# Down products of a feed-forward block ordered by weight part, and the lower activations placed like the upper ones

## The chip, the cores and the metric

One core of a Trainium2 chip runs the whole program. The metric is device time in microseconds for one execution; the median of several runs counts.

## What is computed

Two transformer blocks over 256 tokens of width 1024 in float32, with seven stages: feed-forward, mixer, feed-forward in the first block, then twice a mixer and a feed-forward. Four of the seven are the same gated feed-forward, hidden width 2816:

```python
def _swiglu(x, w_gate, w_up, w_down):
    return (jax.nn.silu(x @ w_gate) * (x @ w_up)) @ w_down
```

The change touches only the last product, with `w_down`, in these four stages.

## The kernel before

**Precision in two parts.** TensorE gets every float32 operand as two tiles: an upper part (`wh`, `hh`, `xh`), which is the rounded copy, and a lower part (`wl`, `hl`, `xl`), which is the rest. A product of two operands is three matmuls: upper by upper, upper activation by lower weight, lower activation by upper weight.

**Weights.** All weights come through one stream (`Stream`, L45 on) in tiles of 128x1024. SP loads a raw tile, ScalarE casts it to `wh` (L89), VectorE subtracts to get `wl` (L94). Four raw tiles and six pairs `wh`, `wl` are in the ring. `take(n)` hands out the next n pairs and issues casts and subtractions for later ones, as far as the ring's pairs are no longer in use. VectorE's subtraction is followed by the load of a later raw tile.

**A feed-forward stage** (`ffn`, L615 on) has a first part and then ten blocks j = 1 to 10 of 256 hidden columns. A block multiplies by the gate weights (`gemm_b2`, lines 535 and 537: weights stationary, activations streamed, 512 and 256 columns), does the same for the up weights, forms silu(gate) x up in `sg`, and splits that into `hh` (ScalarE, L653) and `hl` (VectorE, L654). Then it calls `down` for the chunks of the block before, so that `hh` and `hl` have been ready for a whole block. The engines follow the order in which the code issues work.

**`down`** takes two weight tiles (four in the last call of a stage). The 256 tokens are two halves h, the 1024 output columns two banks b; four PSUM banks add up over the whole stage. Here the activations are stationary (128 columns are loaded into TensorE for each matmul) and 512 columns of weights are streamed. In the old order h is the outer loop, then tile i, then bank b, and for each of these `mm3` (L511 on) issues its three matmuls: (`hh`, `wh`), (`hh`, `wl`), (`hl`, `wh`). All of them are recorded at L523, and so are those of the mixers' products. A call with n=2 has 24. A stage has nine calls with n=2 and one with n=4.

**Places in SBUF.** A spacer of `WL_AT` = 192 bytes lies between the tiles `wh` and `wl`, and one of the same size, `gap3` (L651), between `hh` and `hl`. The other spacers (`gap2` from `HH_AT`, L622) bring `hh` to the same place in each stage. Modulo 512 bytes `wh` and `hh` begin at 160 and `wl` and `hl` at 352 in every feed-forward stage. All offsets within the tiles that a matmul uses are multiples of 512 bytes.

**Three other groups of products** appear in the rows. `gh` is the first product of a mixer, issued all (`xh`, `wh`), then all (`xh`, `wl`), then all (`xl`, `wh`), eight of each for a half of the tokens; in the first mixer `xh` lies at 160 and `xl` at 352. `wo<-hah` are output products of the first mixer, in the old order of three with activations `hah` and `hal`, which both lie at 160. In all of these, weights are streamed, 512 columns at a time, and activations are stationary. `gb` are the gate and up products.

Of the kernel before, what the change touches and what calls it, by code (L numbers as in the profile page):

```python
# [8 lines left out]
F32 = mybir.dt.float32  # L9
# [5 lines left out]
P = 128  # L15
# [12 lines left out]
WL_AT = 192  # L28
# [160 lines left out]
class Kern:  # L189
# [407 lines left out]
    def down(self, accs, chunk, n, act, cut=False):  # L597


        tiles = self.ws.take(n)  # L600
        last = chunk + n == 22
        b2 = [(0, slice(0, 512)), (1, slice(512, D))]
        for h in range(2):
            t = slice(h * P, (h + 1) * P)
            m = n - 2 if last else n
            cs = [b2[0], (2, slice(512, 768)), (3, slice(768, D))] if last and len(accs[h]) > 2 else b2
            for i, (b, c) in [(i, b) for i in range(m) for b in cs] + [(i, b) for b in cs for i in range(m, n)]:
                ah, al = act(chunk + i)
                wh, wl = tiles[i]
                k = chunk + i  # L610
                self.mm3(accs[h][b], [((ah[:, t], al[:, t]), (wh[:, 0, c], wl[:, 0, c]))],
                         k == 0 or b > 1 and i == 0, k == 21 or cut and b == h == 1 and k == 17)


    def ffn(self, gpre, gpost, coef, gnext, hooks=None, cut=False):  # L615
        nc = self.nc
        tt = nc.vector.tensor_tensor
        with self.tc.tile_pool(name="ffn", bufs=3) as fp:
            self.php = fp
            self.pair_xt = True  # L620
            self.nff = getattr(self, "nff", -1) + 1
            fp.tile([P, HH_AT[self.nff] // 4], F32, name="gap2", tag="gap2", bufs=1)  # L622
            hts = {}
            st = {}
            accs = None

            def act(c):
                hh, hl = hts[c // 2]
                return hh[:, c % 2, :], hl[:, c % 2, :]

            def first(h, mid):
                if h == 0:
                    st["w"] = self.ws.take(4)
                p = self.ps(f"fh{h}")
                t = slice(h * P, (h + 1) * P)
                w = st["w"]
                ops = [(self.xh[:, 2 * i + k, t], w[i][x][:, k, :]) for i in range(4) for x in range(2) for k in range(2)]
                ops += [(self.xl[:, k, t], w[k // 2][0][:, k % 2, :]) for k in range(8)]
                for n, (l, r) in enumerate(ops):
                    if mid and n == 24 - 12 // self.after:  # L640
                        mid()
                    nc.tensor.matmul(out=p, lhsT=l, rhs=r, start=n == 0, stop=n == 23)  # L642
                sg = fp.tile([P, S], F32, name="sgf", tag="sgf", bufs=2)
                nc.scalar.activation(out=sg, in_=p[:, 0:S], func=AF.Silu)
                tt(out=sg, in0=sg, in1=p[:, S:2 * S], op=ALU.mult)
                st[h] = sg

            def split(t, j):
                hh = fp.tile([P, 2, S], F32R, name="hh", tag="hh")
                if not hts:  # L650
                    fp.tile([P, WL_AT // 4], F32, name="gap3", tag="gap3", bufs=1)  # L651
                hl = fp.tile([P, 2, S], F32R, name="hl", tag="hl")
                nc.scalar.copy(out=hh, in_=t)  # L653
                tt(out=hl, in0=t, in1=hh.bitcast(F32), op=ALU.subtract)  # L654
                hts[j] = (hh, hl)

            def gather(t, banks):
                for c, p in enumerate(banks):
                    nc.scalar.copy(out=t[:, c, :], in_=p[:, 1, :])  # L659
                    tt(out=t[:, c, :], in0=p[:, 0, :], in1=t[:, c, :], op=ALU.add)  # L660

            self.enter(gpre, first)
            self.pair_xt = False
            self.gain(gnext)
            if gpost:
                self.gain(gpost)
            for j in range(1, 11):
                sg = fp.tile([P, 2, S], F32, name="sg", tag="sg", bufs=1)
                su = fp.tile([P, 2, S], F32, name="su", tag="su", bufs=1)
                gather(sg, self.gemm_b2())  # L670
                nc.scalar.activation(out=sg, in_=sg, func=AF.Silu)
                if j == 1:
                    p = self.ps("ft")
                    for c in range(2):
                        for h in range(2):
                            nc.tensor.transpose(p[:, c * S + h * P:c * S + (h + 1) * P], st[h][:, c * P:(c + 1) * P],
                                                self.ident)
                    split(p.rearrange("p (c t) -> p c t", c=2), 0)
                gather(su, self.gemm_b2())
                tt(out=sg, in0=sg, in1=su, op=ALU.mult)  # L680
                split(sg, j)
                for f in (hooks or {}).get(j, []):
                    f()
                if accs is None:
                    accs = [self.ps2("f0"), self.ps2("f1")]
                if j < 10:
                    self.down(accs, 2 * (j - 1), 2, act, cut)
            if cut:
                accs[1] += [self.ps("f1c")[:, 0:S] for _ in range(2)]
            self.down(accs, 18, 4, act)  # L690
            self.close(accs, gpost, coef)
# [1069 lines left out]
```

## Time and profile before

| what | value |
|---|---|
| median of 3 runs | 1098.65 us (1098.41 to 1099.42) |
| profiled execution, its own time | 1100.22 us |
| its span, first to last instruction | 1098.4 us |
| granted TensorE clock, mean share | 0.998 |
| TensorE busy | 1082.7 us, 99% |
| VectorE, ScalarE, GpSimd busy | 738.0, 598.3, 314.6 us |
| moved by DMA | 190.83 MB, mean 174 GB/s |

The profile is of one execution. Busy shares are means over stages; the chain of work that ended last says which engine's time adds up to the end. Matmuls are pipelined, so the duration of one overlaps the next: what one costs is the interval from its start to the next one's start, which the timeline shows.

### The profile page before, as it was taken

The page shows a single profiled execution, that of the slowest core. Times are in us where ns is not written, and L with a number is a line of the kernel's source. Part 1 is how long each engine was busy: PE and PEld are TensorE (multiplying, and loading weights), DVE is VectorE, ACT ScalarE, POOL GpSimd, SP SyncE. Part 2 cuts the span into 40 slices and gives each one's busy share as a digit, 9 for nine tenths or more (in the row PEclk, how much of TensorE's full clock was granted, in tenths as well). Part 3 has the DMA queues.
Part 4 walks back from the last instruction along what each step waited for, and adds up shares of the span by engine and source line. Part 5 has one row for each costly group of instructions (what it writes and reads, how often), then busy time and mean ns, then how long its engine had stood idle before and what let it go on. Part 6 is the DMA issues. An engine that isn't in the chain of part 4 may idle for free.

```text
span 1098.4 us, 16117 instructions
## 1 busy us (share of the span) xinstructions
PE 1082.7 (99%) x5963; PEld 921.1 (84%) x5963; DVE 738.0 (67%) x1019; ACT 598.3 (54%) x954; POOL 314.6 (29%) x561
## 2 busy tenths in 40 slices
PE   8999999999999999999999999999999999999997
PEld 5888888878878888888987888888889888888886
DVE  5665676889676665667764676757777557565564
ACT  4667555556556554556575554545553465554553
POOL 4005840213310000003023599999505100000000
PEclk9999999999999999999999999999999999999999
DMA  7765565562056655655713665565454346656651
GB/s 237 252 203 179 193 206 176 188 217 75 20 159 226 207 176 193 208 175 185 225 54 100 212 202 177 172 202 181 158 180 160 106 132 196 207 167 203 206 168 63
DMA packets 130256, 190.83 MB, mean 174 GB/s; under 512 B 6017, under 2 KB 101249, under 8 KB 130178
## 3 DMA queue, kind: packets, MB, share of 16 engines
q1 hardware_dynamic: 129440, 187.72, 53.2%
q0 software_dynamic: 736, 2.08, 0.7%
q8 instruction: 47, 0.77, 0.3%
q14 instruction: 31, 0.25, 0.1%
q10 hardware_dynamic: 2, 0.00, 0.0%
HBM read 188.73 MB, written 1.05 MB: 173 GB/s over the span
## 4 chain that ended last, share of the span: by engine, by line
PE 89%; DVE 5%; issue 2%; ACT 1%; POOL 1%; DMA 1%; SPq 0%; POOLq 0%; DVEq 0%; ACTq 0%
PE gb L535 26%; PE f L523 21%; PE gb L537 13%; PE wo L523 5%; PE gb L523 5%; PE fh L642 4%; PE gh L523 3%; PE ga L523 2%; DVE wl L94 1%; PE tp L370 1%; PE lg L523 1%; PE o L888 1%; DMA wraw<-in_w_first_dram 1%; PE M L1382 1%; PE lt L1117 1%
## 5 line engine op out<-in xcount | busy, mean ns | idle before, releaser
L94 DVE TENSOR_TENSOR wl<-wraw,wh 128x1024 fp32r<-128x1024 f32 x338 | 411.6, 1258 | 105.5 <-ACT wh L89 104.4
L535 PE MATMUL gb<-xt,wh 128*128 128x512 f32 x1280 | 439.2, 390 | 0.0
L89 ACT CAST wh<-wraw 128x1024 fp32r<-128x1024 f32 x341 | 345.0, 1047 | 53.6 <-PE f L523 11.3
L537 PE MATMUL gb<-xt,wl 128*128 128x256 f32 x1280 | 353.9, 277 | 0.0
L535 PEld LDWEIGHTS gb<-xt,wh 128*128 128x128 f32 x1280 | 240.3, 188 | 50.7
L537 PEld LDWEIGHTS gb<-xt,wl 128*128 128x128 f32 x1280 | 240.4, 188 | 1.8
L523 PE MATMUL f<-wh,hh 128*128 128x512 f32 x348 | 138.2, 397 | 0.0
L523 PE MATMUL f<-wh,hl 128*128 128x512 f32 x348 | 137.1, 394 | 0.0
L523 PE MATMUL f<-wl,hh 128*128 128x512 f32 x348 | 136.9, 393 | 0.0
L659 ACT COPY sg<-gb 128x256 f32<-128x256 f32 x80 | 29.9, 373 | 142.6 <-PE gb L537 142.5
L660 DVE TENSOR_TENSOR sg<-gb,sg 128x256 f32<-128x256 f32 x80 | 33.2, 422 | 92.2 <-ACT sg L659 91.9
L344 POOL TENSOR_TENSOR v<-ss 128x1 f32<-128x1 f32 x22 | 6.6, 302 | 290.0 <-ACT xs L336 180.8
L523 PEld LDWEIGHTS f<-wh,hl 128*128 128x128 f32 x348 | 65.3, 188 | 16.9 <-DVE hl L654 0.9
L523 PEld LDWEIGHTS f<-wh,hh 128*128 128x128 f32 x348 | 65.4, 188 | 14.6
L523 PEld LDWEIGHTS f<-wl,hh 128*128 128x128 f32 x348 | 65.4, 188 | 13.3
L339 POOL TENSOR_SCALAR ss<-ss 128x1 f32<-128x1 f32 x6 | 2.4, 397 | 234.2 <-ACT xs L336 234.2
L523 PE MATMUL gb<-xt,wh 128*128 128x256 f32 x384 | 69.5, 283 | 0.0
L659 ACT COPY su<-gb 128x256 f32<-128x256 f32 x80 | 29.3, 368 | 65.7 <-PE gb L537 65.7
L523 PEld LDWEIGHTS gb<-xt,wh 128*128 128x128 f32 x384 | 59.4, 189 | 0.4
L523 PE MATMUL gb<-xt,wl 128*128 128x256 f32 x192 | 54.2, 282 | 0.0
L523 PE MATMUL wo<-wh,xt 128*128 128x512 f32 x160 | 52.5, 399 | 0.0
L653 ACT CAST hh<-sg 128x512 fp32r<-128x512 f32 x40 | 24.8, 621 | 50.8 <-DVE sg L680 50.8
(402 smaller groups left out, 1595.1 us busy)
## 6 DMA issues: line engine op xcount, KB each, us to landing
wraw<-in_ffn_w_down_dram SPq DMA_DIRECT2D x88, 512.0 KB, 3.9
wraw<-in_ffn_w_gate_dram SPq DMA_DIRECT2D x80, 512.0 KB, 4.1
wraw<-in_ffn_w_up_dram SPq DMA_DIRECT2D x80, 512.0 KB, 5.5
wraw<-in_ab_w_in_dram SPq DMA_DIRECT2D x20, 512.0 KB, 4.8
wraw<-in_w_qkv_dram SPq DMA_DIRECT2D x18, 512.0 KB, 3.8
wraw<-in_w_first_dram SPq DMA_DIRECT2D x16, 512.0 KB, 4.1
wraw<-in_cd_w_in_dram SPq DMA_DIRECT2D x16, 512.0 KB, 4.2
wraw<-in_w_out_dram SPq DMA_DIRECT2D x8, 512.0 KB, 3.5
```

Source lines behind the costliest of these rows:

```text
L89: self.nc.scalar.copy(out=h, in_=r)
L94: eng.tensor_tensor(out=l, in0=r, in1=h.bitcast(F32), op=ALU.subtract)
L370: nc.tensor.transpose(p[:, j * P:(j + 1) * P], src[:, (b + j) * P:(b + j + 1) * P], self.ident)
L523: self.nc.tensor.matmul(out=out, lhsT=l, rhs=r, start=start and i == 0, stop=stop and i == n - 1)
L535: self.nc.tensor.matmul(out=p, lhsT=wh[:, k % 4, c], rhs=self.x2[:, k, :], start=k == 0, stop=False, skip_group_check=True)
L537: self.nc.tensor.matmul(out=p[:, S:2 * S], lhsT=wl[:, k % 4, c], rhs=self.xh[:, k, :], start=False, stop=k == 7, skip_group_check=True)
L642: nc.tensor.matmul(out=p, lhsT=l, rhs=r, start=n == 0, stop=n == 23)
L653: nc.scalar.copy(out=hh, in_=t)
L659: nc.scalar.copy(out=t[:, c, :], in_=p[:, 1, :])
L660: tt(out=t[:, c, :], in0=p[:, 0, :], in1=t[:, c, :], op=ALU.add)
L888: nc.tensor.matmul(out=o, lhsT=v, rhs=p, start=i % 2 == 0 and n == 0, stop=i % 2 == 1 and n == 5)
L1117: nc.tensor.matmul(out=p[:, 0:384], lhsT=tri[:, 0, :], rhs=s, start=True, stop=False, skip_group_check=True)
```

## The change

In calls of `down` with n=2 the 24 products are issued in three runs of eight: all (`hh`, `wh`), then all (`hl`, `wh`), then all (`hh`, `wl`). Within a run the order is half h, tile i, bank b. In the pairs (x, y) of the new code x picks the activation part and y the weight part, 0 the upper and 1 the lower. The last call of a stage keeps its order. The spacer `gap3` is gone, so `hl` begins at 160 modulo 512 bytes as `hh` does, in all ten calls; `wl` stays at 352.

```diff
@@ def down
         b2 = [(0, slice(0, 512)), (1, slice(512, D))]
+        if not last:
+
+            for x, y in ((0, 0), (1, 0), (0, 1)):
+                for h, i, (b, c) in [(h, i, b) for h in range(2) for i in range(n) for b in b2]:
+                    k = chunk + i
+                    self.nc.tensor.matmul(
+                        out=accs[h][b], lhsT=act(k)[x][:, h * P:(h + 1) * P], rhs=tiles[i][y][:, 0, c],
+                        start=k == x == y == 0, stop=bool(cut and b == h == 1 and k == 17 and y))
+            return
         for h in range(2):
@@ def split
                 hh = fp.tile([P, 2, S], F32R, name="hh", tag="hh")
-                if not hts:
-                    fp.tile([P, WL_AT // 4], F32, name="gap3", tag="gap3", bufs=1)
                 hl = fp.tile([P, 2, S], F32R, name="hl", tag="hl")
```

## Rows read from the trace of the kernel before

**Rows 1.** The page: engine shares, and the granted clock in 40 slices.
```profile
PE 1082.7 (99%) x5963; PEld 921.1 (84%) x5963; DVE 738.0 (67%) x1019; ACT 598.3 (54%) x954; POOL 314.6 (29%) x561
...
PEclk9999999999999999999999999999999999999999
```
**Rows 2.** The page: the chain that ended last, by engine and by line.
```profile
PE 89%; DVE 5%; issue 2%; ACT 1%; POOL 1%; DMA 1%; SPq 0%; POOLq 0%; DVEq 0%; ACTq 0%
PE gb L535 26%; PE f L523 21%; PE gb L537 13%; PE wo L523 5%; PE gb L523 5%; PE fh L642 4%; PE gh L523 3%; PE ga L523 2%; DVE wl L94 1%; PE tp L370 1%; PE lg L523 1%; PE o L888 1%; DMA wraw<-in_w_first_dram 1%; PE M L1382 1%; PE lt L1117 1%
```
**Rows 3.** Windows: us, busy per engine (count), clock, DMA; one call, four groups.
```profile
390.23:395.81 5.57, 5.57 (x26) 4.51 (x25) 3.99 (x5) 3.95 (x5) 0.00 (x0) 1.00 0.45 176
395.81:406.70 10.89, 10.89 (x66) 9.63 (x65) 6.09 (x8) 4.59 (x7) 0.00 (x0) 1.00 0.66 202
```
**Rows 4.** Timeline of TensorE, that call: start us, us, engine, line, tiles, count.
```profile
390.23 0.39 PE L523 MATMUL f<-wh,hh 128*128 128x512 f32 x1
...
395.11 0.40 PE L523 MATMUL f<-wh,hh 128*128 128x512 f32 x1
...
395.81 0.39 PE L535 MATMUL gb<-xt,wh 128*128 128x512 f32 x1
```
**Rows 5.** Timeline of the weight loads in the same call.
```profile
395.11 0.19 PEld L523 LDWEIGHTS f<-wl,hh 128*128 128x128 f32 x1
```
**Rows 6.** Timeline of TensorE, output products of the first mixer, eighteen apart.
```profile
302.41 0.39 PE L523 MATMUL wo<-wh,hah 128*128 128x512 f32 x1
...
306.53 0.39 PE L523 MATMUL wo<-wh,xt 128*128 128x512 f32 x1
```
**Rows 7.** Groups by shape, one tile's groups: count, busy us, mean ns (or min/median/max).
```profile
L523 PE MATMUL f<-wh,hh 128*128 128x512 f32 x348 | 138.2, 397 | 0.0
L523 PE MATMUL f<-wh,hl 128*128 128x512 f32 x348 | 137.1, 394 | 0.0
L523 PE MATMUL f<-wl,hh 128*128 128x512 f32 x348 | 136.9, 393 | 0.0
...
L523 PE MATMUL wo<-wh,hah 128*128 128x512 f32 x16 | 6.3, 393 | 0.0
L523 PE MATMUL wo<-wl,hah 128*128 128x512 f32 x16 | 6.3, 393 | 0.0
L523 PE MATMUL wo<-wh,hal 128*128 128x512 f32 x16 | 6.3, 392 | 0.0
...
L523 PE MATMUL f1c<-wh,hl x8: 279/284/292, 1086.7 to 1091.3; 128*128 128x256 f32 x8
```
**Rows 8.** Timeline of TensorE, first product of the first mixer, runs merged.
```profile
201.92 2.03 PE L523 MATMUL gh<-wl,xt 128*128 128x512 f32 x8
203.79 1.09 PE L523 MATMUL gh<-wh,xt 128*128 128x512 f32 x4
...
207.07 1.78 PE L523 MATMUL gh<-wh,xt 128*128 128x512 f32 x7
208.69 2.03 PE L523 MATMUL gh<-wl,xt 128*128 128x512 f32 x8
210.56 2.02 PE L523 MATMUL gh<-wh,xt 128*128 128x512 f32 x8
```
**Rows 9.** Waits of the weight loads and of ScalarE: us, times, longest us.
```profile
PEld f L523 <- DVE hl L654: 0.9, 4, 0.2
...
ACT wh L89 <- PE f L523: 11.3, 33, 0.4
```
**Rows 10.** Timeline of ScalarE and VectorE during and after the call.
```profile
392.55 3.16 ACT L89 CAST wh<-wraw 128x1024 fp32r<-128x1024 f32 x3
396.05 1.06 ACT L89 CAST wh<-wraw 128x1024 fp32r<-128x1024 f32 x1 [0.35 <-PE f L523]
...
393.62 4.74 DVE L94 TENSOR_TENSOR wl<-wraw,wh 128x1024 fp32r<-128x1024 f32 x4 [0.26 <-ACT wh L89]
399.14 0.42 DVE L660 TENSOR_TENSOR sg<-gb,sg 128x256 f32<-128x256 f32 x1 [0.77 <-ACT sg L659]
```

## The prediction

> **What bounds the kernel now.** I read the page's engine shares first. TensorE is busy 1082.7 of 1098.4 us, and the slices show its granted clock at the upper of its two levels (2.4 GHz) from end to end [rows 1]. The chain of work that ended last is TensorE for 89%, and the third entry of its list by line, `f` L523, is the down products, 21% of the span, some 231 us [rows 2]. VectorE (67%) and ScalarE (54%) are not the bound; whatever they do earlier or later only counts if TensorE waits for it. So I look at how closely the down products follow one another.
>
> A steady stretch of the second feed-forward stage shows it by windows: one call of `down` takes 5.57 us with TensorE busy throughout, and the four gate and up groups behind it 10.89 us, again without a hole [rows 3]. In the timeline the call's first product starts at 390.23 and the first gate product behind it at 395.81: 24 products in 5.58 us, 232.4 ns each [rows 4]. Nothing is waited for; the interval itself is the cost. The weight-load rows add that the load for the next product starts with the current one (both at 395.11) [rows 4, 5], so while one product streams 512 columns of weights, the next product's 128 activation columns are read. This is the only place where an order or an address can act on these intervals.
>
> That the place matters shows in the first mixer's output products `wo<-hah`. They have the same shape and the old order of three (upper by upper, upper by lower weights, lower by upper), but both activation tiles lie at 160 modulo 512. Eighteen of them take from 302.41 to 306.53, 4.12 us, 228.9 ns each [rows 6]. The page's durations say the same: the three forms of `f` last 397, 394 and 393 ns on average, those of `wo<-hah` 393, 393 and 392 [rows 7], 2 ns less for each product.
>
> **The change part by part.** *Count.* The 36 calls with n=2 hold 864 products and the four last calls 204, twelve of them split in two. The page's three groups of 348 and three of 8 in the split bank make 1068 [rows 7]. No product, load, cast or DMA is added or removed; 864 change their order, and in all 1068 `hl` is read at 160 instead of 352 modulo 512.
>
> *First sixteen products of a call (weights `wh` at 160; activations `hh`, then `hl`, both at 160).* Nearest row: the run of upper products in the first mixer's `gh`, the same pair of places in a run. Seven of them take 207.07 to 208.69, 1.62 us, 231.4 each [rows 8]. The other near row is `wo<-hah` with 228.9. I take the middle of the two, 230.2, as neither is nearer: the first has the run, the second the two accumulator banks.
>
> *Last eight products (weights `wl` at 352, activations `hh` at 160).* The lower-weight run in `gh` is exactly this pair in runs of eight: 201.92 to 203.79 and 208.69 to 210.56, 1.87 us each, 233.8 per product [rows 8]. In `wo<-hah` the same pair is one of the three, and costs no more than the others (393 ns) [rows 7]. I take 233.8, as the run is what the change makes, and keep 228.9 for the range.
>
> *Sum for a call.* 16 x 230.2 + 8 x 233.8 = 5554 ns against 24 x 232.4 = 5578 ns: 24 ns less, and 36 calls give 0.86 us. *Last calls.* Their order stays, only `hl` moves, which is the `wo<-hah` case: 2 ns by the durations [rows 7] for some 200 products, 0.4 us; at most (232.4 - 228.9) x 204 = 0.7 us. All of this lies on the chain, so it goes through in full: about 1.3 us.
>
> *Moved reads.* `wl` of a call's first tile is first needed at product 17 instead of 2, `hl` at 9 instead of 3. The only wait that this could save is TensorE's load for `hl`, 0.9 us in four times of at most 0.2 us [rows 9]; that is once a stage, and in the timeline it stands in the stages' last calls, whose order is kept, so I count nothing (0 to 0.2 us gained).
>
> *Moved releases.* `wh` of the first tile is last read at product 14 instead of 18, of the second at 16 instead of 24; `wl` of the first at 22 instead of 17, of the second at 24 instead of 23. Waiting for these buffers are ScalarE's casts and VectorE's subtractions, which fill them for the next block. ScalarE's fourth cast of a batch now waits 0.35 us for the last `f` product (396.05) [rows 10]; it loses that wait. Over the kernel casts wait for `f` 11.3 us in 33 times [rows 9]. VectorE works its four subtractions off from 393.62 in 4.74 us, so the third, which fills the first down tile's `wl`, starts near 396.0, and product 22 is done near 395.5 (start 395.11 plus its 0.4 us). Cover: 0.5 us, and should it fail, the subtraction slips by less than that. Queued behind it is only the addition at 399.14, 0.8 us after the batch ends [rows 10], and the tile is needed by the next call at 406.7, ten microseconds later [rows 3]. SP's loads of the raw tiles are issued behind the subtractions and shift with them, by tenths at most; POOL has no part in this stage. Price on the chain: nothing.
>
> *A rule that speaks against the gain.* The rows show intervals of 228.9 to 233.8 ns for one shape, depending on pair and place [rows 4, 6, 8]. The Trainium skill (TensorE: Matmul & The Clock Gate, Part 2, step by step) says that TensorE has two independent read ports, so loading the next weights takes no read bandwidth from the running product. By that rule neither order nor place would matter and the sum would be zero. The trace doesn't agree fully, as 228.9 and 233.8 stand side by side; but it doesn't show a row where the place alone is changed.
>
> **The rivals.** *A: everything settles at 228.9* as in `wo<-hah`, the lower-weight run too. For it: that row has the same two pairs of places as the new order. Against: `gh`'s lower run at 233.8, twice. Price: 24 x 3.5 ns x 36 = 3.0 us and 0.7 us in the last calls, 3.7 us; 1095.0 us.
>
> *B: the place is not the cause* (it doesn't do what it says): the products follow one another at 232.4 in any order, as a run of 512 columns with a load beside it costs what it costs. For it: `gh`'s upper run (231.4) with both tiles in the same place is hardly better than now. Price 0 to 0.3 us; 1098.6 us.
>
> *C, slower: reloading the same activations is the dear step.* Of the three forms of `f` only upper by upper lasts 397 ns, 2.3 ns above the mean of the three [rows 7], and it alone is followed by a load of the very tile that is in use. Now 8 of 24 products are followed so; in the new order each stationary block serves two banks in a row, 12 of 24. If the dear state holds on through the run, all 24 go to 234.7: 24 x 2.3 x 36 = 2.0 us, and the last calls 0.4 us; 1101.0 us. It decides the sign from a mean interval of 232.4 on. Against: `wo<-hah` has the same reload at 393 ns.
>
> **How the numbers follow.** The profiled execution took 1100.22 us, 1.8 us of it outside the span, and the median of the runs shown is 1098.65, 1.6 below. My sum is a difference of intervals inside the span, so I take it from the median: 1098.65 - 1.3 = 1097.4 us. Chances: forecast 0.52 (1096.4 to 1098.3), A 0.22, B 0.17, C 0.09. About 0.2%, 2.2 us, is what a measurement of this kernel can tell from no change: faster is below 1096.45, slower above 1100.85. Faster gets A and a little of the forecast, 0.25; slower most of C, 0.06; the rest, 0.69, is the same. The range runs from A's 1095.0 to 1099.8, past B and part of the way to C.
>
> **What would show it.** Right: a call near 5.55 us between the first `f` start and the next gate start, its upper products near 230 and its lower-weight run near 233; no new wait of TensorE; ScalarE's fourth cast without its 0.35 us; gate and up groups unchanged at 10.89 us. A shows as 5.49 us a call, B as 5.57, C as 5.63. I am wrong in kind if TensorE waits for `wl`, or if the gate products change.

## The result, and the profile after

The changed kernel takes 1107.74 us (median, 1107.19 to 1108.12) against 1098.85 us (1098.41 to 1099.42) for the kernel before beside it: a ratio of 1.0085, 95% interval 1.0073 to 1.0097. It is slower by 8.9 us. Forecast were 1097.4 us and a range up to 1099.8, so the sign was wrong and the time lies outside the range.

The profiled execution took 1107.95 us, 1106.1 of it span. The page shows the same picture as [rows 1]: TensorE is busy for 99%, at the upper of its clock's two levels throughout, VectorE and ScalarE do a little less than before. In the chain (by line) the two lines of the gate and up products have grown, from 26% and 13% in [rows 2] to 27% and 14%.

```profile
PE 1091.4 (99%) x5963; PEld 928.3 (84%) x5963; DVE 734.0 (66%) x1019; ACT 591.8 (53%) x954; POOL 315.5 (29%) x561
...
PEclk9999999999999999999999999999999999999999
...
PE gb L535 27%; PE f L608 18%; PE gb L537 14%; PE wo L523 5%; PE gb L523 5%; PE fh L651 4%; PE gh L523 3%; PE f L523 3%; PE ga L523 2%; DVE wl L94 1%; PE tp L370 1%; PE lg L523 1%; PE o L895 1%; DMA wraw<-in_w_first_dram 1%; PE M L1389 1%
```

The windows of the block that [rows 3] shows, now cut in three: the call of `down`, the two gate groups, the two up groups. The columns are the stretch, its length, busy time (count) of PE, PEld, DVE, ACT and POOL, granted clock, DMA share, GB/s.

```profile
391.96:397.49 5.53, 5.53 (x27) 4.51 (x25) 3.93 (x5) 4.11 (x6) 0.00 (x0) 1.00 0.44 178
397.49:403.09 5.60, 5.60 (x33) 4.91 (x32) 2.93 (x4) 1.07 (x2) 0.00 (x0) 1.00 0.92 291
403.09:408.69 5.60, 5.60 (x34) 4.92 (x33) 3.12 (x4) 3.16 (x5) 0.00 (x0) 1.00 0.38 100
```

The call has become shorter, 5.53 us instead of 5.58. The loss stands behind it: the four groups take 11.20 us instead of 10.89, with the same products, TensorE busy throughout, the clock granted in full. This holds for all 36 blocks behind a call with n=2: by TensorE's timeline each takes 10.88 or 10.89 us before and 11.20 after. The timeline (start, duration, operation; xN merges N products in a row) shows the call's three runs and the pairs behind it. A pair is one product of 512 columns (L535) and one of 256 (L537).

```profile
391.96 2.01 PE L608 MATMUL f<-wh,hh 128*128 128x512 f32 x8
393.81 1.98 PE L608 MATMUL f<-wh,hl 128*128 128x512 f32 x8
395.62 2.03 PE L608 MATMUL f<-wl,hh 128*128 128x512 f32 x8
397.49 0.40 PE L535 MATMUL gb<-xt,wh 128*128 128x512 f32 x1
397.72 0.28 PE L537 MATMUL gb<-xt,wl 128*128 128x256 f32 x1
397.84 0.40 PE L535 MATMUL gb<-xt,wh 128*128 128x512 f32 x1
...
398.19 0.39 PE L535 MATMUL gb<-xt,wh 128*128 128x512 f32 x1
...
398.54 0.40 PE L535 MATMUL gb<-xt,wh 128*128 128x512 f32 x1
```

A pair now starts every 350 ns: 397.49, 397.84, 398.19, 398.54. It keeps that to the block's end, since 32 pairs of 350 ns are the 11.20 us of the windows. In the kernel before, the pairs behind the same call come every 340 ns (its TensorE timeline, from the second product of the first pair on, which begins at 395.81 [rows 4]):

```profile
396.03 0.28 PE L537 MATMUL gb<-xt,wl 128*128 128x256 f32 x1
396.15 0.39 PE L535 MATMUL gb<-xt,wh 128*128 128x512 f32 x1
...
396.49 0.39 PE L535 MATMUL gb<-xt,wh 128*128 128x512 f32 x1
...
396.83 0.39 PE L535 MATMUL gb<-xt,wh 128*128 128x512 f32 x1
```

The row of L535 over the whole kernel (count: min/median/max of the duration in ns, first and last start) shows that this isn't one block's affair. First the kernel before:

```profile
L535 PE MATMUL gb<-xt,wh x1280: 389/389/478, 27.3 to 1079.8; 128*128 128x512 f32 x183
```

Then the changed one, where the shortest 512-column product (393 ns) lasts longer than the median one did (389):

```profile
L535 PE MATMUL gb<-xt,wh x1280: 393/396/478, 25.8 to 1087.6; 128*128 128x512 f32 x183
```

**The sum.** 36 blocks follow a call with n=2. Each loses 0.31 us in its four groups (11.20 - 10.89): 11.2 us. Each call gains 0.05 us (5.58 - 5.53): 1.8 us back. A last call gains 0.12 us: in the second stage its 48 products run from 488.99 to 499.98 before (first start to last start, 10.99 us) and from 492.32 to 503.19 after (10.87); four of them give 0.5 us. 11.2 - 1.8 - 0.5 = 8.9 us, the difference of the medians. The spans differ by only 7.7 us because this execution reached its first gate product at 25.8 us and that of before at 27.3 (the first starts in the rows above), ahead of any call of `down`; in the opening, the first product of `first` waited 1.34 us for `xt` in that execution of before and 0.17 us in this one.

**So the question** is why products that the change doesn't touch come every 350 instead of 340 ns. The trace of before already holds 350. The first block of a stage has no call of `down` ahead of it, but the 24 products of `first`, which end in a run of eight (`xl`, `wh`). In the second stage of the kernel before its pairs come like this (329.15, 329.50, 329.85, 330.20):

```profile
327.32 2.00 PE L642 MATMUL fh<-wh,xt 128*128 128x512 f32 x8
329.15 0.39 PE L535 MATMUL gb<-xt,wh 128*128 128x512 f32 x1
...
329.50 0.39 PE L535 MATMUL gb<-xt,wh 128*128 128x512 f32 x1
...
329.85 0.40 PE L535 MATMUL gb<-xt,wh 128*128 128x512 f32 x1
...
330.20 0.39 PE L535 MATMUL gb<-xt,wh 128*128 128x512 f32 x1
```

That suggests a theory: the pairs have two steady intervals, and what stands just ahead of them decides which.

### The profile page after: what moved, and what is told of

It is laid out like the page before. It is cut to its first block, busy times and chain, and to the rows that moved or that the text cites. A ratio compares the mean times of both kernels' runs of the same rounds, so it can differ in the third digit from the quotient of the medians.

```text
span 1106.1 us, 16117 instructions
## 1 busy us (share of the span) xinstructions
PE 1091.4 (99%) x5963; PEld 928.3 (84%) x5963; DVE 734.0 (66%) x1019; ACT 591.8 (53%) x954; POOL 315.5 (29%) x561
## 4 chain that ended last, share of the span: by engine, by line
PE 89%; DVE 5%; issue 1%; ACT 1%; POOL 1%; DMA 1%; SPq 0%; POOLq 0%; DVEq 0%; ACTq 0%
PE gb L535 27%; PE f L608 18%; PE gb L537 14%; PE wo L523 5%; PE gb L523 5%; PE fh L651 4%; PE gh L523 3%; PE f L523 3%; PE ga L523 2%; DVE wl L94 1%; PE tp L370 1%; PE lg L523 1%; PE o L895 1%; DMA wraw<-in_w_first_dram 1%; PE M L1389 1%
## 5 line engine op out<-in xcount | busy, mean ns | idle before, releaser
L535 PE MATMUL gb<-xt,wh 128*128 128x512 f32 x1280 | 450.6, 395 | 0.0
L537 PE MATMUL gb<-xt,wl 128*128 128x256 f32 x1280 | 359.7, 281 | 0.0
L89 ACT CAST wh<-wraw 128x1024 fp32r<-128x1024 f32 x341 | 338.5, 1046 | 33.4 <-PE wo L523 8.3
L535 PEld LDWEIGHTS gb<-xt,wh 128*128 128x128 f32 x1280 | 240.4, 188 | 54.4
L537 PEld LDWEIGHTS gb<-xt,wl 128*128 128x128 f32 x1280 | 242.9, 190 | 1.8
L608 PE MATMUL f<-wl,hh 128*128 128x512 f32 x288 | 73.0, 394 | 0.0
L608 PE MATMUL f<-wh,hh 128*128 128x512 f32 x288 | 72.5, 394 | 0.0
L608 PE MATMUL f<-wh,hl 128*128 128x512 f32 x288 | 71.1, 389 | 0.0
L523 PE MATMUL gb<-xt,wh 128*128 128x256 f32 x384 | 69.5, 283 | 0.0
L608 PEld LDWEIGHTS f<-wl,hh 128*128 128x128 f32 x288 | 53.9, 187 | 12.8
L608 PEld LDWEIGHTS f<-wh,hl 128*128 128x128 f32 x288 | 54.1, 188 | 11.4
L608 PEld LDWEIGHTS f<-wh,hh 128*128 128x128 f32 x288 | 51.6, 188 | 10.7
L523 PEld LDWEIGHTS gb<-xt,wh 128*128 128x128 f32 x384 | 59.4, 189 | 0.4
L523 PE MATMUL gb<-xt,wl 128*128 128x256 f32 x192 | 54.2, 282 | 0.0
L523 PE MATMUL wo<-wh,xt 128*128 128x512 f32 x160 | 52.5, 399 | 0.0
L667 DVE TENSOR_TENSOR su<-gb,su 128x256 f32<-128x256 f32 x80 | 33.3, 419 | 28.3 <-ACT su L666 28.3
```

Source lines behind the costliest of these rows:

```text
L89: self.nc.scalar.copy(out=h, in_=r)
L523: self.nc.tensor.matmul(out=out, lhsT=l, rhs=r, start=start and i == 0, stop=stop and i == n - 1)
L535: self.nc.tensor.matmul(out=p, lhsT=wh[:, k % 4, c], rhs=self.x2[:, k, :], start=k == 0, stop=False, skip_group_check=True)
L537: self.nc.tensor.matmul(out=p[:, S:2 * S], lhsT=wl[:, k % 4, c], rhs=self.xh[:, k, :], start=False, stop=k == 7, skip_group_check=True)
L608: self.nc.tensor.matmul(out=accs[h][b], lhsT=act(k)[x][:, h * P:(h + 1) * P], rhs=tiles[i][y][:, 0, c], start=k == x == y == 0, stop=bool( ...
```

## The experiments

In all of them the loop of the new code is written as a list `seq` of products (h, i, b, x, y) that one loop issues in turn; the diffs show how the list is made. "Block" is the steady block of the second stage in each kernel: the call, then the two halves of its four groups.

### Which part of the change, and which spot

Theories of the first round: the handover at the end of the call decides (H); the place of `hl` does (P); the earlier releases of weight buffers bring other work beside the gate products (C).

**Order alone.** The new order, with the spacer back, so that `hl` lies at 352 as before.

```diff
@@ def split, against the kernel after
                 hh = fp.tile([P, 2, S], F32R, name="hh", tag="hh")
+                if not hts:
+                    fp.tile([P, WL_AT // 4], F32, name="gap3", tag="gap3", bufs=1)
                 hl = fp.tile([P, 2, S], F32R, name="hl", tag="hl")
```

> The new order in three runs of eight, with the spacer kept, so the lower activations stay at 352 modulo 512. Theory H (handover): gate and up pairs run in one of two steady states, 340 or 350 ns for a pair of 512 and 256 columns, and the state is taken over from how the call of down before them ends; ending with lower weights (at 352) beside upper activations leads to 350. H expects four groups at 11.20 us, a call of 5.35 to 5.5 us, 1107 to 1110 us. Rival P (place): taking the spacer away is what slows gate and up; it expects 10.89 us for four groups and 1096 to 1098.5 us. Rival C (contention): upper weight tiles come free earlier, so casts and loads run at other times beside gate and up; it expects about what the changed kernel takes, 1107 to 1109 us.

Measured: 1109.33 us against 1098.84, ratio 1.0091 (1.0076 to 1.0106). Block: call 5.54 (H had put it at 5.35 to 5.5), halves 5.60 and 5.60. Its windows:

```profile
392.11:397.65 5.54, 5.54 (x26) 4.51 (x25) 3.96 (x5) 4.13 (x6) 0.00 (x0) 1.00 0.44 175
397.65:403.25 5.60, 5.60 (x34) 4.92 (x32) 2.91 (x4) 1.04 (x2) 0.00 (x0) 1.00 0.91 270
403.25:408.85 5.60, 5.60 (x35) 4.92 (x33) 3.12 (x4) 3.16 (x5) 0.00 (x0) 1.00 0.41 115
```

The whole loss is there with `hl` in its old place. P falls; the order brings the loss. C expected the same time as H here, so this run doesn't tell them apart.

**Place alone.** The old order, without the spacer.

```diff
@@ def down, against the kernel after
             hib = [(h, i, b) for h in range(2) for i in range(n) for b in range(2)]
-            seq = [(*g, x, y) for x, y in ((0, 0), (1, 0), (0, 1)) for g in hib]
+            seq = [(*g, x, y) for g in hib for x, y in ((0, 0), (0, 1), (1, 0))]
```

> The old order of three, without the spacer, so the lower activations lie at 160 modulo 512 as the upper ones. H (handover): the call still ends with a product with upper weights, so four groups stay at 10.89 us; the call falls from 5.57 to 5.50 us as in the first mixer's output products; 1095 to 1098 us. P (place): four groups at 11.20 us, 1106 to 1109 us. C (contention): as before the change, 1098 to 1099 us.

Measured: 1096.91 us against 1098.84, ratio 0.9985 (0.9975 to 0.9994). Its windows:

```profile
387.98:393.51 5.53, 5.53 (x27) 4.51 (x25) 3.94 (x5) 3.95 (x5) 0.00 (x0) 1.00 0.45 181
393.51:398.95 5.44, 5.44 (x34) 4.81 (x32) 2.98 (x4) 1.43 (x2) 0.00 (x0) 1.00 0.92 285
398.95:404.39 5.44, 5.44 (x35) 4.81 (x33) 3.12 (x4) 3.16 (x5) 0.00 (x0) 1.00 0.39 116
```

The place is worth 0.05 us a call (5.53 against 5.58, 2 ns a product); 36 calls give 1.8 us and the last calls some 0.5 us, near the measured 1.9. The groups stay at 340 ns a pair.

**Last two products of a call exchanged, in the kernel before.** A call then ends with a product of the lower weights, as the new order does.

```diff
@@ def down, against the kernel before, calls with n=2
+            hib = [(h, i, b) for h in range(2) for i in range(n) for b in range(2)]
+            seq = [(*g, x, y) for g in hib for x, y in ((0, 0), (0, 1), (1, 0))]
+            seq[-2:] = seq[:-3:-1]
```

> The kernel before, with the last two of the 24 products of each call with n=2 exchanged: it then ends with upper activations by lower weights, as the changed kernel does; nothing else differs. H (handover): four groups at 11.20 us instead of 10.89, 36 blocks, so 10 to 12 us more than before: 1108 to 1111 us. P (place) and C (contention): within 1 us of the kernel before, as neither a place nor a release moves by more than one product.

Measured: 1099.14 us against 1098.84, ratio 1.0001 (0.9991 to 1.001); block 5.57, 5.45 and 5.44. One product of the lower weights at the end is not enough. H in the form "the last product was with lower weights" falls.

**One product of the second run moved to the end, in the kernel after.** All else stays: runs, places, and the releases to within one product, except that the second tile's `wh` and `hl` are last read by the last product instead of the sixteenth.

```diff
@@ def down, against the kernel after
             seq = [(*g, x, y) for x, y in ((0, 0), (1, 0), (0, 1)) for g in hib]
+            seq.append(seq.pop(15))
```

> The changed kernel, with one product of each call with n=2 moved: the last one of the second run (lower activations by upper weights) is issued at the end of the call. H (handover): four groups at 10.89 us, the call between 5.50 and 5.57 us, 1095 to 1098 us. P (place) and C (contention): as the changed kernel, 1107 to 1109 us, four groups at 11.20 us.

Measured: 1096.76 us against 1098.84, ratio 0.9981 (0.9972 to 0.9991). Its windows:

```profile
388.34:393.84 5.50, 5.50 (x26) 4.50 (x25) 3.92 (x5) 3.85 (x5) 0.00 (x0) 1.00 0.46 173
393.84:399.29 5.45, 5.45 (x34) 4.83 (x32) 2.99 (x4) 1.43 (x2) 0.00 (x0) 1.00 0.91 280
399.29:404.73 5.44, 5.44 (x35) 4.83 (x33) 3.12 (x4) 3.16 (x5) 0.00 (x0) 1.00 0.39 114
```

One of 24 products at another spot, and the loss of 8.9 us has become a gain of 2.1. The DMA shares of the halves (0.91, 0.39) are those of the changed kernel (0.92, 0.38), which speaks against C; but ScalarE does a little more beside the first half (1.43 us against 1.07), so C falls for good only with the split of the last product, below. What is decided at the end of the call holds for 32 pairs behind it. Left over is what about the end decides it.

### What about the end

Two theories: a run of products with the lower weights (which lie at 352 modulo 512, the activations at 160) leaves TensorE in the slower state (R), or it is the timing in which the last product leaves off, whatever its tiles, so that a small shift there can flip it (T). T as put on record allows either interval in most of these runs; they can refute R, but hardly T.

**Second and third run exchanged.** The call ends with the run (`hl`, `wh`), both at 160.

```diff
@@ def down, against the kernel after
-            seq = [(*g, x, y) for x, y in ((0, 0), (1, 0), (0, 1)) for g in hib]
+            seq = [(*g, x, y) for x, y in ((0, 0), (0, 1), (1, 0)) for g in hib]
```

> The changed kernel with the second and third run exchanged: upper by upper, then the lower weights, then lower activations by upper weights at the end, both at 160. Two theories for what hands over the state of the gate and up pairs. R (run): a call that ends with two or more products of lower weights (352) beside upper activations (160) leaves the pairs at 350 ns, any other end at 340. T (timing): the state hangs on the timing in which the last product leaves off, and any small shift there can flip it. R expects 340 here: four groups at 10.89 us, a call near 5.50 us, 1094 to 1097 us. T allows 340 or 350; 350 would be about 1106 us.

Measured: 1108.17 us against 1099.28, ratio 1.0082 (1.0067 to 1.0097); block 5.53, 5.60 and 5.60. R falls: no product of the lower weights is near the end, and the pairs still come every 350 ns.

**The run of lower weights first.** A call ends with (`hh`, `wh`), then (`hl`, `wh`).

```diff
@@ def down, against the kernel after
-            seq = [(*g, x, y) for x, y in ((0, 0), (1, 0), (0, 1)) for g in hib]
+            seq = [(*g, x, y) for x, y in ((0, 1), (0, 0), (1, 0)) for g in hib]
```

> The changed kernel with the lower-weight run first: lower weights, upper by upper, lower activations by upper weights. R (run at the end): 340 per pair, four groups at 10.89 us, a call of 5.45 to 5.52 us, 1093 to 1097 us. T (timing): as this ends with the same run of eight as the variant with the lower weights second, the same state as there. If the lower-weight run's 233 ns are a matter of the state it is entered in, it is faster here, 227 to 230 ns per product; if of its places, 233 ns again.

Measured: 1108.25 us against 1099.28, ratio 1.0079 (1.0064 to 1.0094); block 5.53, 5.60 and 5.60. The same again, with eight more products between the lower weights and the gate. The lower-weight run, now entered from gate products, takes 1.86 us (392.47 to 394.33 in the timeline), some 233 ns a product as at the end of a call, so its interval doesn't come from the run ahead of it.

**One product of the second run at the last place but one.** The call still ends with a product of the lower weights.

```diff
@@ def down, against the kernel after
             seq = [(*g, x, y) for x, y in ((0, 0), (1, 0), (0, 1)) for g in hib]
+            seq.insert(22, seq.pop(15))
```

> The changed kernel with the last product of the second run moved to the last place but one, so that one product of lower weights ends the call as in the old order with two products exchanged. R (run): the end is no run of lower weights, so 340 per pair, four groups at 10.89 us, 1095 to 1098 us. T (timing): may be either; 350 and 1107 us would speak against R.

Measured: 1096.81 us against 1099.28, ratio 0.9979 (0.997 to 0.9989); block 5.51, 5.45 and 5.44.

**The last product in two halves of 256 columns.** Order, tiles and places are those of the changed kernel.

```diff
@@ def down, against the kernel after
+                for u, v in ((0, 512),) if j < len(seq) - 1 else ((0, 256), (256, 512)):
                     self.nc.tensor.matmul(
-                        out=accs[h][b], lhsT=act(k)[x][:, h * P:(h + 1) * P], rhs=tiles[i][y][:, 0, c],
+                        out=accs[h][b][:, u:v], lhsT=act(k)[x][:, h * P:(h + 1) * P], rhs=tiles[i][y][:, 0, c0 + u:c0 + v],
```

> The changed kernel with the last product of each call with n=2 done in two of 256 columns: the same operands at the same places in the same order, only the timing of the last product and one more load change. R (run of places at the end): 350 per pair as in the changed kernel, four groups at 11.20 us, 1107 to 1109 us. T (timing): the shift can flip the pairs to 340; then 1096 to 1098 us.

Measured: 1097.0 us against 1099.28, ratio 0.9977 (0.9968 to 0.9987). Its windows:

```profile
388.41:393.92 5.51, 5.51 (x28) 4.55 (x26) 3.93 (x5) 4.10 (x6) 0.00 (x0) 1.00 0.46 184
393.92:399.36 5.44, 5.44 (x34) 4.81 (x33) 2.94 (x4) 1.07 (x2) 0.00 (x0) 1.00 0.94 292
399.36:404.80 5.44, 5.44 (x34) 4.81 (x33) 3.12 (x4) 3.16 (x5) 0.00 (x0) 1.00 0.36 111
```

This tells most. All reads are of the same addresses in the same order up to the last product, and that has the same columns in two instructions. One product more, with its weight load, and 340 takes the place of 350. It is neither which weights come last nor where they lie, but how the last products were issued, as T has it. C falls here: ScalarE and VectorE do the same beside the gate products as in the changed kernel (1.07 and 2.94 us in the first half, against 1.07 and 2.93), and the pairs come every 340 ns all the same.

### Does the state last by itself?

If the interval is a state that holds until something disturbs it, a disturbance in the middle of a block should be able to change it. It was a split in two of the second 512-column product of the up weights.

```diff
@@ def gemm_b2
-                self.nc.tensor.matmul(out=p, lhsT=wh[:, k % 4, c], rhs=self.x2[:, k, :], start=k == 0, stop=False,
-                                      skip_group_check=True)
+                for u, v in ((0, S), (S, 2 * S)) if kick and j == 0 and k == 1 else ((0, 2 * S),):
+                    self.nc.tensor.matmul(out=p[:, u:v], lhsT=wh[:, k % 4, c], rhs=self.x2[:, k, u:v], start=k == 0,
+                                          stop=False, skip_group_check=True)
@@ def ffn
-                gather(su, self.gemm_b2())
+                gather(su, self.gemm_b2(True))
```

**In the kernel after,** where the pairs ahead of the split come every 350 ns.

> The changed kernel, its calls of down untouched; in each block the second product of the up weights (512 columns) is done in two of 256. Theory S (state): the gate and up pairs have two steady states and keep the one they are in until a product of another length or kind disturbs them, whatever the calls of down did. S expects the sixteen pairs of the gate weights at 350 ns and the sixteen behind the split at 340, half of the loss back: 1102 us (1100.5 to 1103.5). Rival W (the call's end, by weights, buffers or bank use, slows what follows for the whole block): 350 in both halves, 1107 to 1109 us.

Measured: 1107.51 us against 1098.58, ratio 1.0083 (1.007 to 1.0097); block 5.51, 5.60 and 5.60. The pairs stayed at 350 ns; the expectation was missed. Either the split changes nothing, or it leads to 350 from wherever it starts. That is told apart by the same split

**in the kernel before,** where they come every 340 ns (the diff above, with the old order and the spacer).

> The kernel before, with the second product of the up weights in each block done in two of 256 columns, as in the changed kernel with the split in mid-block. S in its narrow form (350 is left and 340 entered by any disturbance): all pairs behind it stay at 340, and the first blocks' second halves, now at 350, go to 340; 1098 to 1099.5 us. S in its wide form (a disturbance may flip either way): the pairs behind it may go to 350, then 1104 to 1106 us.

Measured: 1103.68 us against 1098.58, ratio 1.0047 (1.0031 to 1.0062); block 5.57, 5.45 and 5.58. TensorE's timeline around the split, which is the row with x2 (the lines of this kernel are one further down):

```profile
401.49 0.39 PE L536 MATMUL gb<-xt,wh 128*128 128x512 f32 x1
...
401.83 0.39 PE L536 MATMUL gb<-xt,wh 128*128 128x512 f32 x1
...
402.17 0.39 PE L536 MATMUL gb<-xt,wh 128*128 128x256 f32 x2
...
402.51 0.40 PE L536 MATMUL gb<-xt,wh 128*128 128x512 f32 x1
...
402.86 0.39 PE L536 MATMUL gb<-xt,wh 128*128 128x512 f32 x1
...
403.21 0.40 PE L536 MATMUL gb<-xt,wh 128*128 128x512 f32 x1
```

Up to the split and over it, 340 ns (401.49, 401.83, 402.17, 402.51); from then on, 350 (402.51, 402.86, 403.21) to the end of the block. Fourteen pairs of the up weights stand behind the split: 14 x 10 ns x 36 = 5.0 us, against 5.1 measured. A single split has moved the kernel from one interval to the other, and the new one held by itself, as S in its wide form allows (the time lies just under its 1104 to 1106 us); the narrow form falls. So both intervals are states of the same work, and this split leads to the slower from either side.

### The first blocks, and the better versions

The 350 ns of the stages' first blocks (353 on average in the third and fourth stage) should go as well, if what ends `first` is changed: 32 pairs x 10 ns x 4 stages, 1.3 us at most.

**The last product of `first` in two halves, with the call of the version with one product at the last place but one.**

```diff
@@ def first
-                    nc.tensor.matmul(out=p, lhsT=l, rhs=r, start=n == 0, stop=n == 23)
+                    for u, v in ((0, S), (S, 2 * S)) if h == 1 and n == 23 else ((0, 2 * S),):
+                        nc.tensor.matmul(out=p[:, u:v], lhsT=l, rhs=r[:, u:v], start=n == 0, stop=n == 23 and v == 2 * S)
```

> The changed kernel with the last product of the second run as the last but one of the call, and with the last product of the first part of each stage (before the first block) done in two of 256 columns. S expects the first block's pairs, which run at 345 to 352 ns in every kernel so far, at 340 too: 32 pairs, some 10 ns, four stages, about 1.2 us less than without the split there; 1095 to 1096.5 us. If those pairs are slow for another reason (the first block's own waits or loads), 1096.8 us as without it.

Measured: 1096.06 us against 1098.58, ratio 0.9979 (0.997 to 0.9988). The first block stayed at 350 ns, against the expectation: a split last product, which was enough behind a call of `down`, is not enough here. The time lies in the range that S gave, by luck: it can't be told from that of the version without the split.

**A product of upper activations by lower weights moved to the last place but one in `first` too.**

```diff
@@ def first, against the version with one product at the last place but one
                 ops += [(self.xl[:, k, t], w[k // 2][0][:, k % 2, :]) for k in range(8)]
+                if h == 1:
+                    ops.insert(22, ops.pop(15))
```

> The changed kernel with the last product of the second run as the last but one of each call, as in the earlier variant; and in the first part of each stage, which ends with a run of eight equal pairs (lower activations by upper weights), one product of upper activations by lower weights put at the last place but one. If a run of equal pairs at the end is what leaves the gate pairs at 350 ns, and a product of the other kind near the end what brings 340, then the first block's sixteen gate pairs go from 350 to 340, 0.16 us in each of four stages; the sixteen up pairs follow four transposes and stay at 350 or more. 0.6 us less than the variant without it, 1095 to 1096.5 us. If the first part doesn't follow the rule, the gate pairs of the first block stay at 350 and the time is that of the variant without it, 1096 to 1097 us.

Measured: 1096.45 us against 1099.01, ratio 0.998 (0.9971 to 0.9989). In the timeline the first block's gate pairs now come every 340 ns (326.54, 326.88, 327.21 to the rounding):

```profile
326.08 0.39 PE L654 MATMUL fh<-wl,xt 128*128 128x512 f32 x1
326.31 0.39 PE L654 MATMUL fh<-wh,xt 128*128 128x512 f32 x1
326.54 0.39 PE L535 MATMUL gb<-xt,wh 128*128 128x512 f32 x1
...
326.88 0.39 PE L535 MATMUL gb<-xt,wh 128*128 128x512 f32 x1
...
327.21 0.39 PE L535 MATMUL gb<-xt,wh 128*128 128x512 f32 x1
```

In the version that this one starts from, they come every 350 (326.95, 327.30, 327.65):

```profile
326.95 0.39 PE L535 MATMUL gb<-xt,wh 128*128 128x512 f32 x1
...
327.30 0.39 PE L535 MATMUL gb<-xt,wh 128*128 128x512 f32 x1
...
327.65 0.40 PE L535 MATMUL gb<-xt,wh 128*128 128x512 f32 x1
```

The change of the ending works as it does behind a call, in all four stages, and this is the one run that had the rule (run of eight, or another kind near the end) on record before. Its 16 gate pairs x 10 ns x 4 = 0.6 us are too small to be seen in the time; the up pairs of these blocks, which stand behind four transposes, gained nothing. So the state can be set from outside `down`, in another group of products.

**Which version is best.** Six lie at 0.9977 to 0.9985 of the kernel before, and their intervals overlap: the place alone, and every new order that doesn't end in an unbroken run of eight. All beat both kernels. The least edit is the place alone; the new order with a product at the end gains 0.02 to 0.03 us more a call (5.50 and 5.51 against 5.53), about 1 us in all, which these runs can't separate.

## Why the prediction was wrong

**The step that failed** is the one that the prediction hardly argues: "gate and up groups unchanged at 10.89 us". The sum holds a term for each product that the change moves and none for those that it leaves. 36 blocks x 32 pairs x 10 ns = 11.5 us (11.2 by the windows) was missing, three times the 3.7 us of rival A, the largest sum that was weighed. The text itself named what would overthrow it: "I am wrong in kind if TensorE waits for `wl`, or if the gate products change." The second came; no wait did. A premise failed with the step: the overlap of loads and products was called "the only place where an order or an address can act", and it was looked at in the down products alone. The order acted on 32 pairs behind them.

**It could have been seen beforehand.** The working rests on the interval of one shape differing from place to place: 228.9, 231.4, 233.8 ns [rows 4, 6, 8]. That was read as a property of a pair of tiles. The same products, L535 and L537 on the same kinds of tiles, came every 340 ns behind a call and every 350 behind `first`, in the same stage of the trace of before, and the difference lay in what preceded them. The gate pairs of a first block would have given a rival of its own: if the new order's final run of eight acts like that of `first`, 36 x 32 x 10 ns = 11.5 us, less 1.3: 1108.9 us. I had [rows 3] from a steady block only, and took its 10.89 us for the work's own cost.

**The call.** Right in direction, too small: 5.53 us instead of the forecast 5.554, from 5.578. By the starts in its timeline the first sixteen take 391.96 to 395.62, 228.8 ns each, where 230.2 was taken as the middle between 231.4 and 228.9. That they meet the 228.9 of `wo<-hah` [rows 6] is luck: the run (`hh`, `wh`) takes 391.96 to 393.81, 231.3 each, as `gh` had it [rows 8], and the run (`hl`, `wh`) 393.81 to 395.62, 226.3 each, which no row had, though both have both tiles at 160. The last eight take 395.62 to 397.49, 233.8 each, exactly as `gh` had it [rows 8]. The gain is 48 ns a call instead of 24.

**The last calls,** whose order stays: 0.5 us against the forecast 0.4. (Two small readings: their 204 are 192 products of which twelve are split in two, and `f` L523 is the second entry of the list in [rows 2], not the third. Nothing hangs on either.)

**Order and place.** Told apart by the runs, each is worth 40 to 50 ns a call by itself (5.54 with the order alone, 5.53 with the place alone, from 5.58), and both together not more (5.53). The sum had not separated them.

**The rule.** With the place alone changed, a product's interval fell by 2 ns, which is the row that the prediction said was lacking. The Trainium skill (TensorE: Matmul & The Clock Gate, Part 2: What happens when you issue a matmul) says of the two read ports that loading the next tile doesn't take bandwidth from the running product. The runs don't agree with what I had derived from it, that neither order nor place would matter; what in the reads it is, they don't show.

**Moved releases.** Right: nothing on the chain. ScalarE's four casts are now one stretch, without the 0.35 us ahead of the fourth [rows 10], and VectorE's subtractions stand where they did, 3.4 us behind the start of the call. First ScalarE's row, then VectorE's:

```profile
394.28 3.90 ACT L89 CAST wh<-wraw 128x1024 fp32r<-128x1024 f32 x4
...
395.37 4.63 DVE L94 TENSOR_TENSOR wl<-wraw,wh 128x1024 fp32r<-128x1024 f32 x4 [0.27 <-ACT wh L89]
```

**Moved reads.** Right: TensorE has no new wait; the one for `hl` is 1.0 us in four times, as in [rows 9]:

```profile
PEld f L523 <- DVE hl L661: 1.0, 4, 0.2
```

**The rivals.** Of the three, A (5.49 us a call) came nearest to the call, 5.53; the forecast's own 5.554 was nearer. The versions with one product moved reach 5.50 and 5.51. B (place not the cause) is refuted by the place alone. C had the sign, but its mechanism, dearer products within the call, is refuted: a call is shorter in every version of the new order. The case that came was none of them.

**What stays open** is why. Shown is that behind a call of `down` the pairs' interval takes one of two values, that the few products ahead set it, and that it holds until something disturbs it. Which way the disturbance goes I can't foretell: behind `down` a split last product leads to 340 ns, behind `first` it doesn't, and in mid-block it leads to 350. Behind all five endings in a run of eight (the changed kernel, the order alone, the two other orders of the runs, and `first`) it was 350, or 353 on average behind `first` in two stages. In all six with a product of another kind among the last two, it was 340: the kernel before, place alone, exchange, and the moved products in both calls and `first`. This is a rule of these runs. That a run of eight in `down` ends with two loads of the same activations doesn't explain it: in `first` each product of the run loads another block, and it was 350 there too.

Nor do the instructions ahead decide it alone. The up pairs of a stage's first block stand behind four transposes. In the first stage, ahead of any call of `down`, the kernel before and the one with the last two products of a call exchanged issue the same instructions, but four of these pairs take 1.36 us in the trace of the first and 1.40 in that of the second:

```profile
34.07 0.39 PE L535 MATMUL gb<-xt,wh 128*128 128x512 f32 x1
...
35.43 0.39 PE L535 MATMUL gb<-xt,wh 128*128 128x512 f32 x1
```

```profile
33.94 0.39 PE L535 MATMUL gb<-xt,wh 128*128 128x512 f32 x1
...
35.34 0.39 PE L535 MATMUL gb<-xt,wh 128*128 128x512 f32 x1
```

So the same code leads to 340 or 350 ns, which fits a matter of timing. A fixed phase between weight load and running product that repeats from pair to pair could do this; no row shows such a phase, as in both states a load is recorded 2 to 4 ns behind the start of a product.

## What to carry to other kernels

Where TensorE runs without a hole, compare start-to-start intervals of the *same* products at different spots of one trace before costing an edit: where they differ with no wait and the same clock, an edit ahead of them may change their price. Count the products behind a changed stretch as part of the change; here they were 32 pairs for 24 products moved. A long run of equal products handed over to another pattern is worth one trial with a product of another kind among its last two. Here it made the call no longer and was worth 11 us. It has to be measured: a split product helped at one spot, did nothing at another and did harm at a third.

## What the hardware showed that was not expected

- Behind a call, pairs of a 512- and a 256-column product, each with its weight load, run at 340 or 350 ns for whole blocks, at a granted clock of 1.00, with no wait. One product in two instructions at the right spot changes it (1107.74 to 1097.0 us, and the other way 1098.58 to 1103.68).
- Runs of eight equal products also have their own intervals. In a call of the changed kernel they are 231.3 and 226.3 ns for two runs with both tiles at 160 modulo 512, and 233.8 for the lower weights at 352 with activations at 160: the pair of places alone doesn't give the interval.
- The start of the lower activations modulo 512 bytes alone moved the kernel by 1.9 us (0.9985, 0.9975 to 0.9994).
